# All query and key heads made as tile pairs in the projection stage of a gated linear attention encoder layer

## The chip, the cores and the metric

The kernel runs on one core of a Trainium2 chip. The time is the device time of one execution in microseconds (us), as the median of three runs. A profiled execution of the same program has a span (first to last instruction) and a time of its own.

## The reference, cut to what matters

One encoder layer runs over two sequences of 1024 tokens with 1024 features, in float32. For each sequence, with one weight matrix for all twelve projections:

```
h = rmsnorm(x, norm_g) * (1 + scale) + shift          # shift, scale, gate from silu(c) @ w_ada
a_b, a_c, a_x, a_z, q, k, v, b_z, lr_f, lr_b, m_a, m_b = split(h @ w_in)
y_a = (a_b * conv3(a_c * a_x) * silu(a_z)) @ w_a_out
g_f, g_b = log_sigmoid(lr @ w_gate + b_gate) / 16      # one decay per token and key feature
o   = gla(q, k, v, g_f) + reversed gla(q, k, v, g_b)   # 4 heads, 128 key and 256 value features
y_b = (rmsnorm(o) * gla_norm_g * silu(b_z)) @ w_b_out
y   = rmsnorm(x + gate * ((sigmoid(m_a) * y_a + sigmoid(m_b) * y_b) @ w_out))
```

Here gla is linear attention with a decay: token t sees an earlier token s through q_t, the product of the decays between the two, and k_s.

## The kernel before

**Precision.** Each factor of a large product is split into a high and a low part (`split`, L122 a copy on ScalarE, L123 a subtraction on VectorE), and three matmuls hi·hi, hi·lo and lo·hi make one product.

**Two kinds of dense product.** A weight tile gives 128 output features for all 1024 tokens. The plain way, `halves` and `group`, takes 48 matmuls of 512 columns for a tile (2 token halves, 8 blocks of the inner dimension, 3 parts), 96 for two tiles. `halves` hands them out in 4 steps of 12 matmuls; `group` takes two tiles at once and hands out one step for each of the 8 inner blocks. The pair way, `fast`, takes two tiles together by a Strassen-like scheme with 7 products of 12 matmuls, 84 for two tiles; `stationary` makes the 7 combined weight operands (VectorE and ScalarE) and, in the first sequence, also stores them in `kept_d`, from which `loaded` fetches them for the second sequence. Results are put together by VectorE and ScalarE behind each product.

**Stages.** For each sequence, `projections` runs a list of pair jobs: convolution tiles first, then one pair of Q tiles (heads 0 and 1), one pair of K tiles, four pairs each of V and of the gate b_z, four pairs of m_a. Beside the jobs behind the convolutions it hands out a side chain, `decays`, and in the second sequence `gate_rows`: `owed` grows with each product of a job, and a step of the chain is issued whenever it passes one. `decays` has a yield between its steps; for each head it loads `wg` and `lrs` from DRAM, then one step later multiplies them (L851), and works out the decays T over six more steps. The small product that `lrs` comes from is `low_ranks` (L818, 32 matmuls). `mixers` then runs the four heads of `attention`; between its parts it issues steps of dense products on the plain path, in proportion to a written length of each part (`LENGTHS`): first `gates` (Q and K tiles of heads 2 and 3, 16 steps; six m_b tiles, 24 steps; the last two as a `group`, 8 steps), then `first_out` (32 steps), which reads back the eight convolution results `ta_d` through `reload` (each in two halves, through the six `raw` buffers, split into eight of the 18 `big` buffers). That is 80 steps, 20 for a head. `merge` and, at the end, `final` follow.

**Inside a head.** `attention` loads T, q and k, forms own-token products, then goes through 7 levels: a ScalarE copy (L920), matmuls (L892), and VectorE work on the products and on Q, K and T (L925, L933, L936, L938). Behind the levels come transposes, states and outputs with short VectorE work.

**What sets the order.** A list scheduler places instructions on each engine's queue, by the order in which the program issues them and by its own estimate of when their inputs are ready; an engine then works through its queue in that order. Loads of weights get a higher priority (`load_w`). In the opening, `queue` fixes the order of loads by hand.

Of the kernel before, what the change touches and what calls it, by code (L numbers as in the profile page):

```python
# [11 lines left out]
F32 = mybir.dt.float32  # L12
# [5 lines left out]
P = 128  # L18
D = 1024
KT = D // P  # L20
# [37 lines left out]
def encoder_kernel(ctx, tc, x_p, x_s, x_t, weights, w_lr, w_gate, w_out, vectors, b_gate, final_norm_g, masks, y_p, y_s):  # L58
# [44 lines left out]
    kept_d = dram.tile([36, 7, P, 2 * HALF], F32, name="kept_d")  # L103
# [250 lines left out]
    def run(steps):  # L354
        for _ in steps:
            pass
# [59 lines left out]
    def start(mv):  # L416
# [12 lines left out]
        nc.scalar.activation(out=consts[:, 5:6], in_=sc[:, 0, :1], func=AF.Abs_reciprocal_sqrt, bias=eps)  # L429
# [4 lines left out]
        def tokens(i):  # L434

            sq = big("sq")
            for b in range(2):
                queue(nc.sync.dma_start(out=xT[i][:, b, :], in_=x_t[0, i + 4 * b]))
                nc.scalar.activation(out=sq[:, b, :], in_=xT[i][:, b, :], func=AF.Square)
            last = i == KT // 2 - 1  # L440
            if not last:
                nc.vector.tensor_add(out=sq[:, 0, :], in0=sq[:, 0, :], in1=sq[:, 1, :])
            over_features([sq[:, b, :] for b in range(1 + last)], lambda t: sums[t], i == 0, last)
# [150 lines left out]
    def projections(s, mv, started):  # L594
# [100 lines left out]

        for w, d in ((W_Q, q_d), (W_K, k_d)):
            jobs.append(out_job(w, [d[s][r, :, 0, :] for r in range(2)]))
# [7 lines left out]
        if not started:  # L705
            run(low_ranks(s, mv))
            more = last_conv_jobs(0)
            jobs = more + jobs
            n_conv += len(more)
        steps = 7 * (len(jobs) - n_conv)  # L710
        side = chain(decays(s), gate_rows() if s else ())
        n_side = (1 + 8 * NH) + (KT + 1 + 2 if s else 0)
        owed = 0.0
        for n, _ in enumerate(fast(jobs, mv)):
            if n + 1 >= 7 * n_conv:
# [34 lines left out]
    def mixers(s, mv):  # L750
        def gates():
            for w, d in ((W_Q, q_d), (W_K, k_d)):
                for h in range(2, NH):
                    sg = small("sg")
                    yield from halves(w + h, lambda ps, sl: nc.scalar.copy(out=sg[:, sl], in_=ps), mv.act)
                    nc.scalar.dma_start(out=d[s][h, :, 0, :], in_=sg)
# [13 lines left out]
            yield from group([(W_MA + i, gate(i)) for i in range(n, n + 2)], mv.act)  # L770

        def first_out():
            act = reload(ta_d[s])
# [21 lines left out]
        dense, each = chain(gates(), first_out()), (2 * KT + 4) * 4.0 / NH  # L795
        owed = 0.0
# [30 lines left out]
    def decays(s):  # L827
# [12 lines left out]
        for h in range(NH):  # L840
            wg, lrs = small("wg", F32R, (96, 2, P)), small("lrs", F32R, (96, L))
            nc.sync.dma_start(out=wg.bitcast(F32), in_=wg_d[:, :, h * P:(h + 1) * P])
            nc.sync.dma_start(out=lrs.bitcast(F32), in_=lr_d[s])
            yield
# [362 lines left out]
```

## Time and profile before

| | us |
|---|---|
| median of 3 runs | 2380.84 (2375.48 to 2383.9) |
| the profiled execution, its own time | 2388.54 |
| its span | 2386.7 |
| PE busy in the span | 2300.6 |
| DVE (VectorE) busy | 1422.5 |
| ACT (ScalarE) busy | 1002.8 |

PE is TensorE, PEld its weight loads, DVE VectorE, ACT ScalarE, POOL GpSimd and SP the queue that issues most loads. Matmuls overlap in the pipeline, so the duration of one is longer than the distance to the next, and a busy PE can still be slower than its best. PEclk is the clock granted to TensorE, 1.00 for 2.4 GHz and 0.50 for 1.2 GHz. L123 is line 123 of the kernel.

By the first instruction of each head on VectorE (L885), the heads of the first sequence begin at 673.6, 762.5, 851.7 and 957.7 us, those of the second at 1746.9, 1833.2, 1922.3 and 2029.3 us. L955, the first VectorE instruction behind the levels, falls at 804.2 us in the second head of the first sequence, and at 907.6 us in the third.

### The profile page before, as it was taken

How to read it: one execution, taken by the hardware profiler on the slowest of the kernel's cores; microseconds unless marked ns; L12 is line 12 of the kernel's file. 1: busy time of each engine (PE TensorE's matmuls, PEld its weight loads, DVE VectorE, ACT ScalarE, POOL GpSimd, SP SyncE). 2: the span in 40 equal slices, each digit the busy share in tenths (PEclk: the TensorE clock that was granted, in tenths of full speed). 3: DMA queues.
4: the chain of work that ended last, by engine and by line, in shares of the span. 5: the costliest groups of instructions: out<-in, count | busy, mean ns of one | idle time of the engine just before them, and what ended most of it. 6: DMA issues, size and time to landing. Idle time of an engine off the chain costs nothing.

```text
span 2386.7 us, 29259 instructions
## 1 busy us (share of the span) xinstructions
PE 2300.6 (96%) x10897; PEld 1882.3 (79%) x10897; DVE 1422.5 (60%) x2021; ACT 1002.8 (42%) x1652; POOL 35.7 (1%) x72
## 2 busy tenths in 40 slices
PE   7999999999989989999899999999999989999998
PEld 3688887887878877888688888878788868888887
DVE  4666776666676787967632332333576776955443
ACT  4543333566745545543421113544245444442221
POOL 0000000000000000000000000000000000000000
PEclk9999999999999999999999999999999999999999
DMA  6167767888853245565356666778854144468431
GB/s 236 67 250 278 269 256 279 308 302 304 315 203 137 76 144 202 210 236 198 113 203 212 210 207 225 258 255 278 293 192 154 58 157 167 153 232 308 157 124 62
DMA packets 189902, 494.63 MB, mean 207 GB/s; under 512 B 18912, under 2 KB 45632, under 8 KB 185664
## 3 DMA queue, kind: packets, MB, share of 16 engines
q1 hardware_dynamic: 166960, 405.98, 49.2%
q10 hardware_dynamic: 22800, 86.78, 9.5%
q8 instruction: 86, 1.41, 0.2%
q14 instruction: 56, 0.46, 0.1%
HBM read 294.90 MB, written 197.79 MB: 206 GB/s over the span
## 4 chain that ended last, share of the span: by engine, by line
PE 81%; DVE 7%; DMA 6%; ACT 3%; issue 1%; SPq 1%; POOL 0%; DVEq 0%; POOLq 0%; ACTq 0%
PE ps L141 9%; PE ps L143 9%; PE ps L142 9%; PE pl L277 8%; PE pl L278 8%; PE pl L279 8%; PE ps L277 6%; PE ps L278 6%; PE ps L279 6%; PE pl L892 2%; DMA raw<-in_weights_dram 2%; PE pm L141 1%; PE pm L142 1%; PE pm L143 1%; PE pm L413 1%
## 5 line engine op out<-in xcount | busy, mean ns | idle before, releaser
L123 DVE TENSOR_TENSOR w<-raw,w 128x512 fp32r<-128x512 f32 x298 | 201.9, 686 | 124.7 <-ACT w L122 123.6
L122 ACT CAST w<-raw 128x512 fp32r<-128x512 f32 x298 | 183.8, 621 | 143.6 <-PE ps L143 44.3
L277 PE MATMUL pl<-th,w 128*128 128x512 f32 x584 | 227.8, 390 | 0.0
L278 PE MATMUL pl<-tl,w 128*128 128x512 f32 x584 | 227.5, 390 | 0.0
L279 PE MATMUL pl<-th,w 128*128 128x512 f32 x584 | 227.4, 389 | 0.0
L141 PE MATMUL ps<-b,w 128*128 128x512 f32 x512 | 203.8, 398 | 16.0 <-ACT w L122 16.0
L142 PE MATMUL ps<-b,w 128*128 128x512 f32 x512 | 201.9, 394 | 0.0
L143 PE MATMUL ps<-b,w 128*128 128x512 f32 x512 | 201.9, 394 | 0.0
L141 PE MATMUL ps<-hi,w 128*128 128x512 f32 x432 | 173.2, 401 | 1.7 <-ACT hi L390 1.7
L282 ACT COPY keep<-pl 128x512 f32<-128x512 f32 x116 | 67.6, 583 | 254.8 <-PE pl L279 254.7
L143 PE MATMUL ps<-hi,w 128*128 128x512 f32 x432 | 172.1, 398 | 0.0
L142 PE MATMUL ps<-lo,w 128*128 128x512 f32 x432 | 171.2, 396 | 0.7 <-DVE lo L391 0.7
L277 PE MATMUL ps<-hi,w 128*128 128x512 f32 x352 | 137.6, 391 | 0.8 <-ACT w L122 0.8
L278 PE MATMUL ps<-lo,w 128*128 128x512 f32 x352 | 137.7, 391 | 0.0
L279 PE MATMUL ps<-hi,w 128*128 128x512 f32 x352 | 137.6, 391 | 0.0
L277 PEld LDWEIGHTS pl<-th,w 128*128 128x128 f32 x584 | 109.7, 188 | 23.9 <-ACT keep L282 0.7
L278 PEld LDWEIGHTS pl<-tl,w 128*128 128x128 f32 x584 | 109.8, 188 | 22.9
L279 PEld LDWEIGHTS pl<-th,w 128*128 128x128 f32 x584 | 109.8, 188 | 22.9
L141 PEld LDWEIGHTS ps<-b,w 128*128 128x128 f32 x512 | 97.3, 190 | 34.8 <-ACT w L122 16.6
L143 PEld LDWEIGHTS ps<-b,w 128*128 128x128 f32 x512 | 97.0, 189 | 19.9 <-DVE w L123 0.5
L892 PEld LDWEIGHTS pl<-Q,km 128*128 128x128 f32 x768 | 94.3, 196 | 22.0 <-ACT km L920 11.1
L142 PEld LDWEIGHTS ps<-b,w 128*128 128x128 f32 x512 | 97.2, 190 | 18.1
(288 smaller groups left out, 5041.6 us busy)
## 6 DMA issues: line engine op xcount, KB each, us to landing
kept_d<-w SPq DMA_DIRECT2D x196, 512.0 KB, 4.0
raw<-in_weights_dram SPq DMA_DIRECT2D x256, 256.0 KB, 4.3
w<-kept_d SPq DMA_DIRECT2D x112, 512.0 KB, 3.7
wk<-kept_d SPq DMA_DIRECT2D x168, 256.0 KB, 3.1
g<-g_d SPq DMA_DIRECT2D x32, 512.0 KB, 4.8
araw<-in_weights_dram SPq DMA_DIRECT2D x16, 512.0 KB, 3.8
ta_d<-u ACTq DMA_DIRECT2D x16, 512.0 KB, 3.6
v_d<-single ACTq DMA_DIRECT2D x16, 512.0 KB, 4.9
```

Of the source, the lines that this page charges most:

```text
L122: high = nc.scalar.copy(out=hi, in_=raw)
L123: engine.tensor_sub(out=lo, in0=raw, in1=hi.bitcast(F32))
L141: nc.tensor.matmul(out, ahi, bhi, start=(first and i == 0), stop=False)
L142: nc.tensor.matmul(out, ahi, blo, start=False, stop=False)
L143: nc.tensor.matmul(out, alo, bhi, start=False, stop=(last and i == n - 1))
L277: nc.tensor.matmul(ps, whi[:, cs], mhi, start=(first and k == 0), stop=False, skip_group_check=True)
L278: nc.tensor.matmul(ps, whi[:, cs], mlo, start=False, stop=False, skip_group_check=True)
L279: nc.tensor.matmul(ps, wlo[:, cs], mhi, start=False, stop=(k == 3), skip_group_check=True)
L282: nc.scalar.copy(out=job[i, "keep"], in_=ps)
L413: nc.tensor.matmul(ps[:2, :2 * P], sc[:, :, 4 * kg + k], raw[:, k, :], start=(kg + k == 0), stop=(kg * k == 3))
L892: nc.tensor.matmul(pl[:, j * P:(j + 1) * P], km[:, c * P:(c + 1) * P], qm(c), start=True, stop=True)
```

## The change

- The Q and K tiles of heads 2 and 3 leave `gates` (16 steps of the plain path for each sequence) and become two more pair jobs in `projections`: 16 pair jobs behind the convolutions in place of 14, and four more entries in `kept_d`.
- `mixers` has 64 dense steps in place of 80, 16 for a head, and begins with `owed = 2.0`.
- The reload of the convolution results moves from the start of `first_out` into the last `group` of `gates`: two tiles behind each of its last four steps.
- `decays` gets one more yield between the loads of `wg` and `lrs` and their first use; the side chain's count goes from 8 to 9 steps a head.
- In the second sequence, `low_ranks` is issued behind the ninth product of the pair jobs, not ahead of the first.
- In the opening, the first Square (L439) must follow the one-element Abs_reciprocal_sqrt (L429), and so the Sigmoid ahead of that one.

```diff
-    kept_d = dram.tile([36, 7, P, 2 * HALF], F32, name="kept_d")
+    kept_d = dram.tile([40, 7, P, 2 * HALF], F32, name="kept_d")
...
-        nc.scalar.activation(out=consts[:, 5:6], in_=sc[:, 0, :1], func=AF.Abs_reciprocal_sqrt, bias=eps)
+        table = nc.scalar.activation(out=consts[:, 5:6], in_=sc[:, 0, :1], func=AF.Abs_reciprocal_sqrt, bias=eps)
...
-                nc.scalar.activation(out=sq[:, b, :], in_=xT[i][:, b, :], func=AF.Square)
+                square = nc.scalar.activation(out=sq[:, b, :], in_=xT[i][:, b, :], func=AF.Square)
+                if i + b == 0:
+                    after(square, table)
...
         for w, d in ((W_Q, q_d), (W_K, k_d)):
-            jobs.append(out_job(w, [d[s][r, :, 0, :] for r in range(2)]))
+            for h in range(0, NH, 2):
+                jobs.append(out_job(w + h, [d[s][h + r, :, 0, :] for r in range(2)]))
...
         if not started:
-            run(low_ranks(s, mv))
             more = last_conv_jobs(0)
...
-        n_side = (1 + 8 * NH) + (KT + 1 + 2 if s else 0)
+        n_side = (1 + 9 * NH) + (KT + 1 + 2 if s else 0)
         owed = 0.0
         for n, _ in enumerate(fast(jobs, mv)):
+            if s and n == 8:
+                run(low_ranks(s, mv))
...
         def gates():
-            for w, d in ((W_Q, q_d), (W_K, k_d)):
-                for h in range(2, NH):
-                    sg = small("sg")
-                    yield from halves(w + h, lambda ps, sl: nc.scalar.copy(out=sg[:, sl], in_=ps), mv.act)
-                    nc.scalar.dma_start(out=d[s][h, :, 0, :], in_=sg)
...
-            yield from group([(W_MA + i, gate(i)) for i in range(n, n + 2)], mv.act)
+
+            for k, _ in enumerate(group([(W_MA + i, gate(i)) for i in range(n, n + 2)], mv.act)):
+                if k >= 4:
+                    reload(ta_d[s], conv, (2 * k - 8, 2 * k - 7))
+                yield
+
+        conv = [None] * KT
 
         def first_out():
-            act = reload(ta_d[s])
+            def act(k, sl):
+                return conv[k][:, 0, sl], conv[k][:, 1, sl]
...
-        dense, each = chain(gates(), first_out()), (2 * KT + 4) * 4.0 / NH
-        owed = 0.0
+        dense, each = chain(gates(), first_out()), 2 * KT * 4.0 / NH
+        owed = 2.0
...
             nc.sync.dma_start(out=lrs.bitcast(F32), in_=lr_d[s])
+            yield
             yield
             t1, t2 = big("t1"), big("t2")
```

## Rows read from the trace of the kernel before

**Rows 1.** Windows (start:end, length, busy us and count by engine), undisturbed projections of both sequences.

```profile
440.00:540.00 100.00, 100.00 (x443) 82.70 (x442) 67.72 (x95) 59.08 (x80) 0.00 (x0) 1.00 0.86 321
...
1180.00:1460.00 280.00, 280.00 (x1237) 231.86 (x1236) 86.96 (x93) 52.88 (x76) 0.00 (x0) 1.00 0.60 205
```

**Rows 2.** Windows: PE, PEld, DVE, ACT, POOL, then PEclk, DMA share; heads in two stretches.

```profile
762.50:804.20 41.70, 41.41 (x232) 35.08 (x230) 38.78 (x51) 19.03 (x32) 0.00 (x0) 1.00 0.39 147
804.20:851.70 47.50, 46.99 (x276) 39.94 (x275) 27.07 (x48) 25.52 (x60) 2.40 (x4) 1.00 0.28 94
851.70:907.60 55.90, 43.05 (x221) 35.47 (x220) 48.35 (x67) 27.90 (x48) 0.00 (x0) 0.88 0.56 198
907.60:957.70 50.10, 48.97 (x285) 41.32 (x284) 38.55 (x69) 29.64 (x68) 3.02 (x4) 1.00 0.49 165
...
1922.30:1979.30 57.00, 44.62 (x220) 37.02 (x219) 48.45 (x68) 27.61 (x48) 0.00 (x0) 0.85 0.55 194
```

**Rows 3.** Windows of the dense products' tile ps alone (PE, PEld, DVE, ACT), second head.

```profile
762.50:804.20 41.70, 29.61 (x120) 22.02 (x120) 0.00 (x0) 2.83 (x5) 1.00 0.39 147
804.20:851.70 47.50, 30.99 (x122) 21.78 (x122) 0.00 (x0) 3.10 (x6) 1.00 0.28 94
```

**Rows 4.** Groups by line of VectorE, 762.5 to 804.2 us: weight splits.

```profile
L123 DVE TENSOR_TENSOR w<-raw,w 128x512 fp32r<-128x512 f32 x5 | 3.4, 686 | 0.0
```

**Rows 5.** The chain of waits: PE, the whole span; us in total, times, longest.

```profile
PE ps L141 <- ACT w L122: 16.0, 2, 8.3
PE pm L851 <- DMA lrs<-lr_d: 11.1, 4, 3.8
PE pm L413 <- POOL sc L426: 7.4, 1, 7.4
PE pl L370 <- ACT Xh L122: 6.9, 2, 6.7
...
PE pm L1035 <- DVE ot L1027: 5.7, 11, 0.6
...
PE ps L818 <- ACT hi L122: 4.1, 1, 4.1
```

**Rows 6.** Groups by line of VectorE, 851.7 to 907.6 us: splits of the reload.

```profile
L123 DVE TENSOR_TENSOR b<-raw,b 128x512 fp32r<-128x512 f32 x16 | 10.6, 683 | 0.0
```

**Rows 7.** Waits of the SP queue, 851 to 907 us.

```profile
SPq L117 <- DVE b L123: 28.4, 12, 8.1
```

**Rows 8.** Windows (columns as in Rows 2) around the four waits for lrs.

```profile
400.00:420.00 20.00, 16.40 (x66) 13.09 (x65) 10.31 (x15) 6.98 (x12) 0.00 (x0) 0.91 0.91 314
540.00:560.00 20.00, 17.58 (x71) 14.01 (x70) 9.32 (x15) 12.39 (x20) 0.00 (x0) 0.91 0.80 294
1560.00:1580.00 20.00, 16.22 (x65) 12.90 (x64) 2.07 (x3) 3.59 (x6) 0.00 (x0) 0.91 0.81 263
1620.00:1640.00 20.00, 18.74 (x83) 15.20 (x82) 4.43 (x5) 12.49 (x16) 0.00 (x0) 1.00 0.79 255
```

**Rows 9.** Timeline of ScalarE in the opening: start, us, instruction.

```profile
7.55 1.06 ACT L439 ACTIVATE sq<-xT 128x1024 f32<-128x1024 f32 x1 [5.55 <-DMA xT<-in_x_t_dram]
8.63 1.28 ACT L425 ACT_TABLE_LOAD   x1
...
11.06 1.28 ACT L429 ACT_TABLE_LOAD   x1
...
12.56 5.77 ACT L439 ACTIVATE sq<-xT 128x1024 f32<-128x1024 f32 x6
```

**Rows 10.** Timeline of PE in the opening.

```profile
10.46 6.28 PE L413 MATMUL pm<-araw,sc 128*2 128x256 f32 x16 [7.44 <-POOL sc L426]
...
22.54 7.11 PE L370 MATMUL pl<-sq,ones 128*128 128x512 f32 x12 [1.64 <-DVE sq L442]
```

**Rows 11.** Page, DMA issues: count, KB each, median us to landing.

```profile
v_d<-single ACTq DMA_DIRECT2D x16, 512.0 KB, 4.9
```

**Rows 12.** Windows (columns as in Rows 2), two us inside the third head's wait.

```profile
896.00:898.00 2.00, 0.00 (x0) 0.00 (x0) 0.22 (x1) 0.00 (x0) 0.00 (x0) 0.50 1.02 349
```

## The prediction

> **What bounds the kernel now.** I read the share of each engine first, then windows stage by stage, then the waits of TensorE, then single stretches. TensorE is the bound nearly everywhere: in undisturbed stretches of the projections it never pauses, with 443 matmuls in 100 us or 1237 in 280 us [rows 1]. That is 0.226 us from one to the next, and it is the price of a 512-column matmul in all that follows (a single one is shown as 0.39 us, because neighbours overlap). VectorE and ScalarE have room there: 67.7 and 59.1 us of 100 in the first sequence, far less in the second.
>
> The heads of the attention are different, and the reader should see two stretches in each [rows 2]. From the head's first VectorE instruction to the end of the levels, 41.7 us in the second head, VectorE is busy for 38.8 us (93%) and TensorE for 41.4: both are full. From there to the next head, 47.5 us, VectorE is busy for 27.1 us only and TensorE for 47.0. The dense steps are spread evenly: 120 matmuls in the first stretch and 122 in the second [rows 3], about what the program's written lengths ask for (43 of 83 parts of 240). So the scheduler does not run dense work ahead to any extent that shows.
>
> **What leaves and what comes, on TensorE.** Four more pair jobs (two for each sequence) are 4 x 84 = 336 matmuls, at 0.226 us +76.0 us, all in stages where TensorE has no gap to hide them. VectorE and ScalarE keep up with such jobs today [rows 1], so I add nothing for the operands and the stores. Eight tiles leave the attention, 8 x 48 = 384 matmuls, 86.9 us if TensorE stays the bound there. On TensorE alone the change is worth 10.9 us.
>
> **What the attention gives back.** Each of eight heads loses 48 matmuls, about 24 in each stretch. In the second stretch VectorE leaves 20 us free, so 24 x 0.226 = 5.4 us come back, 43 us over eight heads. In the first VectorE is as full as TensorE; all that comes back is what the missing tile asked of VectorE: two splits of 0.686 us a head, half of them in this stretch [rows 4], 0.7 us, 5.5 us in all. TensorE will then idle for some 4.7 us in each first stretch. Lower bound 49 us, upper bound 87 us if the scheduler lets later dense steps run ahead into the gaps and the second stretch shrinks in turn. I take the lower one, because the even counts of [rows 3] show no run-ahead. From it I take 6 us: in the second stretch TensorE already waits for the scaled output, 5.7 us in 11 waits [rows 5], each behind a few dense matmuls, and with a fifth fewer of them I let these waits double. Net -43 us.
>
> **The reload.** The third heads last 106.0 and 107.0 us against 88.9 to 89.2 for undisturbed neighbours (from the heads' first instructions), 17 us too long each. In their first stretches, 55.9 and 57.0 us, VectorE works for 48 us and TensorE is at a mean clock of 0.88 and 0.85 [rows 2]. The cause: 16 reload splits, 10.6 us of VectorE [rows 6], fall into the stretch where it has nothing to spare, and the first weights of `first_out` wait in SP's queue behind raw buffers that these splits hold (28.4 us in 12 waits [rows 7]). TensorE then stands for 8.3 us and again in the second sequence, 16.0 us together [rows 5]. After the change the four reload steps are dense steps 29 to 32; with 16 a head and a start of 2 they fall at (29-2)/16 = 1.69 to 1.88 heads, in the second stretch of the second head. There VectorE has 20 us free for 11 us, and the buffers of the projections' operands come free one pair with each step. What may still be late is the weights of `first_out`, four raws behind sixteen in the same six buffers, issued in the last step; and the loads of T, q and k for the third head queue on SP behind them. I let 5 us of the 17 stay in each sequence: -25 us. Bounds: -10 (the weights are still as late as a whole wait of 8 us) and -34.
>
> **The decays.** At four places TensorE waits for `lrs`, 11.1 us in all, 3.8 the longest [rows 5]. The matmuls missing around them, against 89 in 20 us, are 23, 18, 24 and 6 [rows 8], 71 x 0.226 = 16 us, because the granted clock is lower behind each wait (0.91 on average in three of the windows). The added yield gives the loads one more side step. There are 48 or 37 steps for 112 products, so one in 2.3 to 3.0 products of 2.7 us: 6.3 to 8 us more, above the longest wait. I take -15. Bounds: -8 (half of the waits move on with the load, which can itself be late on SP) and -16. The same chain has `gate_rows`; its spacing hardly changes and I leave its waits alone.
>
> **The opening.** The Sigmoid stands behind the first Square, which waits until 7.55 us for its data, and behind a table load of 1.28 us; a second one comes at 11.06 [rows 9]. So `sc` is late and TensorE starts the conditioning product at 10.46 us, after 7.4 us of waiting [rows 5, 10]. With the small functions first, that product can start some 4 us earlier, and both table loads are gone from among the squares; the last square can end little earlier, as its data arrive late. The sums end at 29.7 us today [rows 10] and everything behind follows them. I take -5, between 0 and -7.
>
> **Low ranks and the start of the heads.** Moving `low_ranks` takes away 32 matmuls (7.2 us) with which TensorE partly fills the time until the last normalised tile is there; it waits for that tile inside them now (4.1 us [rows 5]). Other products of the first pairs can take part of the place: +2, between -3 and +5. Its weights take one of four operand buffers for some products; the pair jobs have six operands made ahead, so I add nothing. At the first head of the first sequence TensorE waits 6.7 us for the own-token operand [rows 5]; `owed = 2.0` puts two more dense steps (5.4 us) ahead of it, but the queue already holds three there. -2, between 0 and -5.
>
> **The sum.** 76 - 43 - 25 - 15 - 5 + 2 - 2 = -12 us. Against the profiled execution's own 2388.5 that is 2376.5; the median shown lies 7.7 us below that execution, so I forecast 2369 us. A change of 0.3%, 7 us, is about what a measurement of this kernel can tell from none.
>
> **The rivals.**
> *The dense work runs ahead.* The scheduler fills the gaps of the first stretches, and nearly all of the 87 us come back: 38 to 44 us more than I count, about 2328 us. For it: ahead of the first head's own products, TensorE did run dense steps while it waited. Against it: [rows 3].
> *The reload stays a stall.* The move doesn't do what it says, since the weights of `first_out` still come behind the reload's raws in SP's queue [rows 7], or T, q and k behind both; then the 25 us are not gained: 2394 us, slower. It decides from 12 us of 25 on.
> *Small buffers run short.* `wg` and `lrs` hold two of six `small` buffers for a side step longer, while two to four hold results on their way out and one the temporary of a silu. When none is free, the copy out of a product waits, and TensorE behind it. A store needs 4.9 us to land [rows 11]; one such wait for each of eight head loads is 39 us: 2408 us. It decides from 1.5 us a load on. Against it: the waits of TensorE list none on a store.
> *The clock.* Inside the long waits the granted clock fell to 0.50, that is 1.2 GHz [rows 12], while the many short waits in the second head went with 1.00 [rows 2]. If the gaps of 4.7 us a head, spread over seven levels, bring the lower level, one first stretch at 1.2 GHz doubles some 36 us of TensorE's work (41.4 less 24 matmuls), 31 us longer after its slack; one in eight is enough to be slower, 2400 us. The Trainium skill ("TensorE: Matmul & The Clock Gate", section "A second HAM failure mode: psum-queue depth-cycling") says that brief idling between groups of matmuls, if frequent, can make the clock swing between its levels; by that rule this rival would be the likeliest case. The trace doesn't bear it out so far: 11 waits of up to 0.6 us fell in stretches at 1.00.
>
> **How the numbers follow.** Forecast 0.46, within 2356 to 2382 by its own bounds; run-ahead 0.22; reload stays 0.12; small buffers 0.10; clock 0.04; 0.06 for what I don't see. Faster by over 0.3% (under 2373.7) are two thirds of the first, all of the second and a few others: 0.58. Same: the rest of the first, some of the third: 0.21. Slower 0.21. The range of 8 in 10 reaches from the run-ahead case to the reload that stays: 2328 to 2395.
>
> **What would show it.** Right: heads with 96 dense matmuls in each stretch, a first stretch still near 41 us with TensorE idle for 4 to 5, a second near 42; third heads below 92 us; no wait for `lrs`; the conditioning product starting before 7 us; two jobs more of 19 us in each projection stage. Wrong: first stretches with 110 or more dense matmuls and heads near 79 us (run-ahead); TensorE still waiting for the weights of `first_out`; new waits on stores in the projections; a clock below 1.00 in the levels.

## The result and the profile after

The changed kernel takes 2400.2 us (median of 4 runs, 2395.3 to 2401.2), against 2382.37 for the kernel before on the same chip. The medians are 17.8 us apart; the ratio over the runs is 1.0064, with a 95% interval of 1.0048 to 1.008, which is some 15 us. It is slower, where 12 us less was forecast, and it lies outside the range. Its profiled execution has a span of 2397.6 us, 10.9 more than the one before, which was itself 6 us above its median.

The page after, its head:

```profile
span 2397.6 us, 29218 instructions
...
PE 2304.7 (96%) x10849; PEld 1885.0 (79%) x10849; DVE 1435.3 (60%) x2043; ACT 995.6 (42%) x1645; POOL 36.0 (1%) x72
```

Cut at the same events in both traces (first pair product, first VectorE instruction of the first head, last VectorE output of the last head, first pair product of the next projections or first product of `final`), the spans divide as follows.

| stage | before, us | after, us | difference |
|---|---|---|---|
| opening, to the first pair product | 118.3 | 114.5 | -3.8 |
| projections, first sequence | 555.3 | 586.5 | +31.2 |
| attention, first sequence | 375.2 | 357.3 | -17.9 |
| merge, first sequence | 89.3 | 83.5 | -5.8 |
| projections, second sequence | 608.9 | 643.3 | +34.4 |
| attention, second sequence | 372.3 | 349.4 | -22.9 |
| merge, second sequence | 85.5 | 81.4 | -4.1 |
| final | 181.9 | 181.6 | -0.3 |

The projections grew by 65.6 us, and attention and merge gave back 50.7. One thing lies between the two: in the kernel before, the low-rank product of the second sequence begins 84.0 us into the 89.3 of the first merge row, so 5.3 us of that row's 5.8 are the moved product, which the kernel after has in its projections. Counted with that product in the projections both times, these grew by 60 us, where the sum had 63 (76 - 15 + 2), and attention and merge gave back 45, where it had 70 (43 + 25 + 2). Nearly the whole error stands in that one place. That the projections come so near is luck in part: the runs below show two of their terms off in opposite directions. The windows of the kernel after, with the columns of [rows 2], show what its attention stage is made of; the first two lines are the two attention stages, then come seven of its sixteen stretches:

```profile
701.10:1058.40 357.30, 322.62 (x1806) 273.33 (x1806) 294.72 (x452) 187.68 (x383) 10.48 (x16) 0.95 0.43 153
1785.10:2134.50 349.40, 321.35 (x1804) 272.49 (x1804) 283.33 (x433) 175.09 (x361) 10.50 (x16) 0.96 0.40 141
...
743.80:785.50 41.70, 40.94 (x246) 34.91 (x245) 27.41 (x49) 23.75 (x57) 2.44 (x4) 1.00 0.29 101
785.50:826.80 41.30, 40.56 (x233) 33.85 (x232) 39.32 (x54) 20.66 (x34) 0.00 (x0) 1.00 0.34 128
826.80:876.60 49.80, 42.42 (x239) 36.14 (x238) 34.32 (x62) 29.26 (x71) 2.52 (x4) 0.93 0.57 195
876.60:921.40 44.80, 40.85 (x230) 35.01 (x228) 42.90 (x60) 23.34 (x38) 0.00 (x0) 0.96 0.37 137
921.40:969.20 47.80, 42.73 (x238) 35.61 (x238) 37.92 (x68) 28.27 (x65) 2.40 (x4) 1.00 0.58 190
...
1013.10:1058.40 45.30, 32.44 (x166) 27.71 (x165) 34.67 (x61) 24.83 (x60) 3.12 (x4) 0.77 0.42 140
2089.10:2134.50 45.40, 33.33 (x166) 28.39 (x165) 34.58 (x61) 24.81 (x60) 3.12 (x4) 0.77 0.41 139
```

The reader should see three things. The third head's first stretch did fall, from 55.9 us [rows 2] to 44.8. The second head's second stretch did not: 47.5 us before [rows 2], 49.8 now, though it holds fewer dense matmuls. And the last heads' second stretches take 45 us with TensorE busy for 32 or 33 of them. The dense products alone (tile ps) in those two last stretches:

```profile
1013.10:1058.40 45.30, 8.75 (x35) 6.08 (x34) 2.61 (x4) 0.00 (x0) 0.77 0.42 140
2089.10:2134.50 45.40, 8.69 (x35) 6.21 (x34) 2.75 (x4) 0.00 (x0) 0.77 0.41 139
```

33 of these 35 begin inside the stretch, where an even spread has 96, and only 7 and 8 of them are dense steps of the attention stage, all in its first 2 us. The other 26 and 25 are products of merge, behind a pause of some 30 us. The dense work has run ahead and is used up; what lasts is the chain of short steps of the last head alone. TensorE's clock falls there (columns as above):

```profile
1015.00:1020.00 5.00, 0.87 (x7) 0.78 (x7) 5.00 (x6) 2.02 (x4) 0.00 (x0) 0.98 0.26 105
1020.00:1033.00 13.00, 10.17 (x42) 8.66 (x41) 9.03 (x22) 5.79 (x15) 0.00 (x0) 0.50 0.11 42
```

TensorE was busy for 0.87 us of 5 before the clock fell to 1.2 GHz, and then worked for 10.17 of 13 us at that level.

The head of the list of TensorE's waits, after, whole span:

```profile
PE pm L1041 <- DVE ot L1033: 23.5, 12, 4.7
PE pm L977 <- DVE kt L123: 8.3, 2, 4.1
PE pl L370 <- ACT Xh L122: 6.9, 2, 3.7
PE pl L370 <- DVE sq L444: 4.6, 2, 3.0
```

The waits for `lrs` (11.1 us) and for the first weights of `first_out` (16.0 us) of [rows 5] are gone. In their place TensorE waits 23.5 us for the scaled output `ot`, 5.7 before [rows 5]; the three longest waits are now for steps of the heads' own chain. The cause in the second head is seen in the groups of VectorE from 826.8 to 876.6 us (first its busy time, then the idle time before and what ended it) and in the issues of SP there:

```profile
L123 DVE TENSOR_TENSOR b<-raw,b 128x512 fp32r<-128x512 f32 x16 | 10.6, 685 | 0.8 <-ACT b L122 0.7
...
L1033 DVE TENSOR_TENSOR ot<-ot,ors 128x1024 f32<-128x1024 f32 x2 | 2.4, 1224 | 6.0 <-POOL ors L363 6.0
```

```profile
837.86 12.03 SPq L117 DMA_DIRECT2D raw<-ta_d  x10
851.36 6.20 SPq L117 DMA_DIRECT2D raw<-in_weights_dram  x6
859.43 2.94 SPq L117 DMA_DIRECT2D raw<-in_x_t_dram  x3
862.42 0.90 SPq L782 DMA_DIRECT2D g<-g_d  x2
863.72 0.32 SPq L883 DMA_DIRECT2D T<-t_d  x1
866.15 0.32 SPq L885 DMA_DIRECT2D qk<-q_d  x1
```

All 16 splits of the reload fall into this one stretch, where the prediction had put them, between the short VectorE steps on which the states and outputs wait. Behind the reload on SP come weights, the next normalisation's input, and only then T and q of the third head, whose first ScalarE step waits 6.4 us for q.

### The profile page after: what moved, and what is told of

Same layout as the page of the kernel before. It is cut to its first block, busy times and chain, and to the rows that moved or that the text cites. A ratio compares the mean times of both kernels' runs of the same rounds, so it can differ in the third digit from the quotient of the medians.

```text
span 2397.6 us, 29218 instructions
## 1 busy us (share of the span) xinstructions
PE 2304.7 (96%) x10849; PEld 1885.0 (79%) x10849; DVE 1435.3 (60%) x2043; ACT 995.6 (42%) x1645; POOL 36.0 (1%) x72
## 4 chain that ended last, share of the span: by engine, by line
PE 79%; DVE 7%; DMA 6%; ACT 4%; issue 2%; POOL 1%; SPq 0%; DVEq 0%; ACTq 0%; POOLq 0%
PE ps L141 9%; PE ps L143 9%; PE ps L142 9%; PE pl L279 8%; PE pl L277 8%; PE pl L278 8%; PE ps L279 6%; PE ps L278 6%; PE ps L277 6%; PE pl L898 3%; DMA raw<-in_weights_dram 3%; PE pm L141 1%; PE pm L142 1%; PE pm L143 1%; PE pl L370 1%
## 5 line engine op out<-in xcount | busy, mean ns | idle before, releaser
L277 PE MATMUL pl<-th,w 128*128 128x512 f32 x624 | 244.6, 392 | 0.3 <-ACT keep L282 0.3
L279 PE MATMUL pl<-th,w 128*128 128x512 f32 x624 | 244.2, 391 | 0.0
L278 PE MATMUL pl<-tl,w 128*128 128x512 f32 x624 | 244.0, 391 | 0.0
L279 PE MATMUL ps<-hi,w 128*128 128x512 f32 x376 | 146.5, 390 | 0.4 <-DVE w L123 0.4
L278 PE MATMUL ps<-lo,w 128*128 128x512 f32 x376 | 146.5, 390 | 0.4 <-DVE lo L123 0.4
L277 PE MATMUL ps<-hi,w 128*128 128x512 f32 x376 | 146.5, 390 | 0.4 <-ACT hi L122 0.4
L277 PEld LDWEIGHTS pl<-th,w 128*128 128x128 f32 x624 | 117.8, 189 | 26.3 <-ACT keep L282 0.9
L278 PEld LDWEIGHTS pl<-tl,w 128*128 128x128 f32 x624 | 117.9, 189 | 24.7
L279 PEld LDWEIGHTS pl<-th,w 128*128 128x128 f32 x624 | 117.8, 189 | 24.7
L141 PE MATMUL ps<-hi,w 128*128 128x512 f32 x304 | 123.4, 406 | 1.7 <-ACT hi L390 1.7
L142 PE MATMUL ps<-lo,w 128*128 128x512 f32 x304 | 121.3, 399 | 0.7 <-DVE lo L391 0.7
L143 PE MATMUL ps<-hi,w 128*128 128x512 f32 x304 | 121.1, 398 | 0.0
```

The source lines that it names most:

```text
L141: nc.tensor.matmul(out, ahi, bhi, start=(first and i == 0), stop=False)
L142: nc.tensor.matmul(out, ahi, blo, start=False, stop=False)
L143: nc.tensor.matmul(out, alo, bhi, start=False, stop=(last and i == n - 1))
L277: nc.tensor.matmul(ps, whi[:, cs], mhi, start=(first and k == 0), stop=False, skip_group_check=True)
L278: nc.tensor.matmul(ps, whi[:, cs], mlo, start=False, stop=False, skip_group_check=True)
L279: nc.tensor.matmul(ps, wlo[:, cs], mhi, start=False, stop=(k == 3), skip_group_check=True)
```

## The experiments

Two theories stood after the comparison. The first: the heads are bound by their own chain once 16 dense steps a head are left, so that what is taken off TensorE or VectorE there comes back only in part. The second: the heads could be shorter, but something of the change is badly placed (the reload, the raw buffers, dense work that runs ahead). Ratios are to the kernel before, on the same chip, with 95% intervals.

### Which part costs what

**The pairs alone** on the kernel before (the jobs, the steps taken out of `gates`, `each`):

```diff
-            jobs.append(out_job(w, [d[s][r, :, 0, :] for r in range(2)]))
+            for h in range(0, NH, 2):
+                jobs.append(out_job(w + h, [d[s][h + r, :, 0, :] for r in range(2)]))
...
-        dense, each = chain(gates(), first_out()), (2 * KT + 4) * 4.0 / NH
+        dense, each = chain(gates(), first_out()), 2 * KT * 4.0 / NH
```

> The kernel before with only the Q and K tiles moved into pair jobs (64 dense steps, start of 0; reload, decays, opening and low ranks as before). Theory A, the attention gives back about half of the 87 us that leave it while the four jobs cost 76: 2405 to 2420 us, with the third heads' stall still there. Rival B, the pairs pay and one of the moved parts costs: 2360 to 2378 us.

Measured: 2408.1 us, 1.0102 [1.0081, 1.0122]. The projections grow by 34.1 and 34.7 us (68.8, against 76 by count), attention and merge fall by 43.8 together. So the pairs lose some 25 us by themselves, and the rest of the change gives only 9 of them back. The two attention stages, with the columns of [rows 2], and the wait for `lrs` that is left:

```profile
708.70:1072.50 363.80, 325.84 (x1803) 274.20 (x1802) 295.90 (x452) 188.53 (x383) 10.35 (x16) 0.94 0.43 151
1801.00:2149.40 348.40, 320.62 (x1815) 271.09 (x1814) 284.10 (x433) 175.91 (x362) 10.89 (x16) 0.96 0.40 141
```

```profile
PE pm L847 <- DMA lrs<-lr_d: 3.9, 2, 3.6
```

The last line tells why the jobs cost 69 us and not 76. In the projections, TensorE's busy time grows by 74 us (1142 to 1216), near the count; its pauses shrink by 5.5, as the side chain's steps are spread over 112 products of jobs in place of 98, and the waits for `lrs` fall from 11.1 us [rows 5] to 3.9.

Two things more stand in this trace. The reload's splits fall between 876 and 895 us, behind the start of the third head, and the wait for the first weights of `first_out` stays (14.3 us). And neighbouring heads overlap: the third head's first VectorE instruction comes at 860.3 us, 23.9 behind the end of the second head's levels, while the second head's last output follows at 883.6. So the length of a head from start to start (68.7 us here, then 122.9) belongs to the order that the scheduler chose; the stages are no shorter for it.

**The small parts alone** (opening, extra yield, moved low-rank product):

> The kernel before with the opening's order, the added yield of the decays and the moved low ranks, and nothing else. Theory A: the waits for lrs (16 us with the slow clock) and some 5 us of the opening go: 2355 to 2365 us. Rival B, these parts cost as much as they bring: 2376 to 2390 us.

Measured: 2374.8 us, 0.9957 [0.9943, 0.9971], 10 us less, where the prediction's terms make 18. By these ratios the pairs and the small parts make 1.0059 together, and the whole change 1.0064: the moved reload and the owed start, which were to bring 27 us, brought nothing that can be measured.

**The yield alone:**

```diff
-        n_side = (1 + 8 * NH) + (KT + 1 + 2 if s else 0)
+        n_side = (1 + 9 * NH) + (KT + 1 + 2 if s else 0)
...
             nc.sync.dma_start(out=lrs.bitcast(F32), in_=lr_d[s])
             yield
+            yield
```

> The kernel before with only the added yield of the decays and its count. The prediction's term: 15 us less, ratio 0.9937, the waits for lrs gone. Rival: the three small parts together gave 10 us, of which the opening is 4 by its stage, and one wait for lrs was still there (2.4 us); so 6 to 8 us, ratio 0.997, and the waits are shorter rather than gone, for lrs is late on SP by more than one side step.

Measured: 0.9978 [0.9969, 0.9988], 5 us less. Its waits of TensorE:

```profile
PE ps L141 <- ACT w L122: 15.2, 2, 8.7
...
PE pm L370 <- ACT gp L122: 5.4, 1, 5.4
...
PE ps L277 <- ACT w L205: 3.2, 1, 3.2
PE pm L852 <- DMA lrs<-lr_d: 3.1, 1, 3.1
```

Three of the four waits for `lrs` are gone (11.1 us before [rows 5], 3.1 now), but two others have come, which the kernel before does not list among its longest: 5.4 us for the operand of `gate_rows`, issued from the same side chain, and 3.2 us for a pair job's operand. Both fall in the projections. The prediction had left `gate_rows` alone.

**The changed kernel without the four added jobs** (queries and keys of heads 2 and 3 are not made; those of heads 0 and 1 are read):

> The changed kernel without the four added pair jobs: Q and K of heads 2 and 3 are not made, and those of heads 0 and 1 are read in their place. By the sum, 4 x 84 matmuls of 0.226 us: 76 us less than the changed kernel, 2324 us. If jobs cost more than their matmuls (operands, stores, the side chain): 2315 us or less. If part of them filled waits: 2332 us or more.

Measured: 2335.6 us, 0.981 [0.9781, 0.984]: 61 us below the kernel after by the ratios, 64 by its projections (559.0 and 606.9 us). The jobs cost 61 to 69 us in these runs, not 76. Without them, waits like those of the yield alone stand in the projections (5.4 us for `gate_rows`, 3.5 for a pair job's operand, 2.5 for `lrs`), which are 1.1 us or less in the kernel after.

### Whether dense work that runs ahead starves the last head

**Dense steps held back:** the first matmul of a dense step must follow the last matmul that attention issued before it.

```diff
+        if not pe["dense"]:
+            pe["mine"] = made
+        elif pe["due"]:
+            after(made, pe["mine"])
+            pe["due"] = False
```

> The changed kernel with an order on TensorE's queue: no dense step of the attention stage stands ahead of the attention matmuls issued before it. Theory A, dense work run ahead starves the last head (31 dense matmuls in its second stretch, TensorE idle for 22 us): the last heads get some 100 dense matmuls back and end 4 to 8 us sooner each, while TensorE idles more in first stretches: 2385 to 2395 us. Rival C, the second stretches are bound by their own chain whatever the filling: 2398 to 2410 us.

Measured: 2456.6 us, 1.0305 [1.0276, 1.0333]. The last heads do get about 200 dense matmuls each, but the heads last 89.7 to 101.6 us, where they had 83.9 to 92.6. TensorE's waits, first two lines:

```profile
PE pl L140 <- ACT Xh L122: 31.8, 8, 5.0
PE pl L140 <- ACT km L940: 21.8, 16, 3.5
```

Held back in this way, dense matmuls no longer cover the latencies of the chain. Running ahead is not the fault.

**More work for the last head:** the first 72 matmuls of merge, with the reload of six tiles that they need, become six more dense steps, 17.5 for a head in place of 16; they are the last ones, at the end of the last head.

```diff
-        dense, each = chain(gates(), first_out()), 2 * KT * 4.0 / NH
+        dense, each = chain(gates(), first_out(), first_merge()), (2 * KT * 4.0 + 6) / NH
```

> The changed kernel, with the first 72 matmuls of merge (two output tiles over the first six inner blocks, and the reload of those blocks) issued as 6 more dense steps in the last head. Theory A: they fill idle time of the last head's second stretch, 16 us for each sequence less what the reload adds: 2370 to 2382 us. Rival C, TensorE's idle time there is not to be had because ScalarE, VectorE or the buffers hold the reload back: 2395 us or more.

Measured: 2441.1 us, 1.0235 [1.0215, 1.0255]. The last heads grow from 89.1 and 89.6 us to 99.3 and 94.9, and the two attention stages by 40 us together. TensorE also waits 18.2 us for copies of a reload, right behind the last heads, where merge has lost the products that it began with. TensorE's idle time in the last head was not to be had in this way, for work that needs VectorE and ScalarE as well.

### Whether the reload stands in the wrong place

**The reload back at the start of `first_out`**, the rest as after:

> The changed kernel with the reload of the convolution results back at the start of first_out, all else as changed. Theory D, the moved reload brings nothing because its loads, copies and splits hold up the second head's states and the third head's loads instead of first_out's weights: 2395 to 2408 us, within 6 us of the changed kernel. Rival, the move is worth the 25 us that the sum gave it and something else is lost: 2420 us or more.

Measured: 2394.5 us, 1.0049 [1.003, 1.0068], against 1.0064 for the kernel after: the move gains nothing that can be measured. The scheduler puts the reload into the second head's second stretch anyway (47.0 us; its splits fall between 849 and 867).

**Without raw buffers:** each tile is loaded whole into the low half of its big buffer and split in place, so that SP never waits for a raw buffer there.

```diff
-            for t in range(2):
-                sl = slice(t * HALF, (t + 1) * HALF)
-                split(b[:, 0, sl], b[:, 1, sl], staged(src[k][:, sl]), nc.vector)
+            whole = b.bitcast(F32)[:, 1, :]
+            nc.sync.dma_start(out=whole, in_=src[k])
+            split(b[:, 0, :], b[:, 1, :], whole, nc.vector)
```

On the kernel after:

> The changed kernel, but reload (that of merge too) loads each tile whole into the low half of its own big buffer and splits it there: no raw buffers and half the loads on SP, and one copy and one subtraction of 1024 columns in place of two of 512. Theory D1, the queue of SP and the six raw buffers are what holds up the neighbours: 2375 to 2390 us. Theory D2, the work on ScalarE and VectorE in between the states is: 2393 to 2402 us.

Measured: 2395.9 us, 1.0059 [1.0043, 1.0076]; the second stretch is 50.4 us. The same edit on the kernel before:

> The kernel before with the same reload without raw buffers, at its old place. If the wait of the third heads comes from first_out's weights behind the raw buffers of the reload, some 8 us for each sequence go: 2362 to 2374 us. If it comes from VectorE being full in that stretch, as much of the stall stays: 2376 to 2386 us.

Measured: 2370.6 us, 0.9958 [0.9943, 0.9973]. The third heads fall from 106.0 and 107.0 us to 99.9 and 99.8, and the wait for the first weights of `first_out` is gone from the list. So the queue of raw buffers cost something before, and nothing after.

**Without the split at all,** in the reload of the convolution results alone:

```diff
+            if any(src is d for d in ta_d):
+                for part in range(2):
+                    nc.sync.dma_start(out=b.bitcast(F32)[:, part, :], in_=src[k])
+                tiles[k] = b
+                continue
```

On the kernel after, before, and on the pairs alone:

> The kernel after, but the reload of the convolution results copies each tile by DMA into both halves of its big buffer; the split into high and low parts (16 copies on ScalarE and 16 subtractions on VectorE for each sequence) and the raw buffers are left out, so the low part is wrong data. The reload of merge keeps its split. Theory E (the engine work lengthens the chain at whatever place it stands): the second heads' second stretch falls from 49.8 and 49.7 us to some 42, the third heads' first from 44.8 to some 42, and the third heads lose the wait for q: 8 + 4 us for each sequence, about 2376 us, ratio 0.997 to before. Rival T (what is late is the transfers and SP's queue, the engines' work is hidden): 2394 to 2402 us, ratio 1.005 to 1.008, with second stretches still near 50 us.

> The kernel before with the same edit (no split in the reload of the convolution results). If the reload's work was the cause of the long third heads, as the prediction had it, they fall from 106 and 107 us to some 90, 34 us in all: 2350 us, ratio 0.986. If the transfers are the cause, they fall little: 2370 to 2382 us. The difference between this run and the kernel before is the reload's price there; the same difference for the kernel after, by theory E some 24 us, is what is left of it behind the move. The prediction had 34 and 9.

> The pairs alone, with the reload of the convolution results copied by DMA into both halves of its buffers; the split of it is left out, so the low part is wrong data. Theory F (the two gains are not additive): the reload's price is some 8 us here, as in the kernel after, so 2400 us, ratio 1.007. Rival (another part of the change makes the price small, and the terms add): 26 us, as in the kernel before, 2382 us, ratio 0.999.

Measured: after 1.0045 [1.0032, 1.0057], before 0.989 [0.9874, 0.9906], pairs alone 1.0119 [1.0095, 1.0143]. The windows of both attention stages, in this order: the kernel before, then it without the split; after, without the split (with it, above); the pairs alone, without the split.

```profile
673.60:1048.80 375.20, 352.23 (x1976) 297.50 (x1977) 300.68 (x460) 197.54 (x399) 11.13 (x16) 0.97 0.44 152
1746.90:2119.20 372.30, 355.35 (x1987) 299.88 (x1986) 288.06 (x439) 183.80 (x376) 9.60 (x16) 0.98 0.40 141
```

```profile
669.30:1030.90 361.60, 350.15 (x1982) 295.42 (x1981) 291.67 (x444) 188.43 (x383) 10.73 (x16) 1.00 0.48 170
1724.20:2083.60 359.40, 351.94 (x1986) 297.17 (x1985) 278.81 (x423) 175.22 (x360) 9.60 (x16) 1.00 0.44 157
```

```profile
708.90:1064.20 355.30, 324.03 (x1806) 273.34 (x1805) 285.67 (x436) 179.97 (x367) 10.36 (x16) 0.96 0.46 166
1786.10:2131.20 345.10, 318.25 (x1802) 269.50 (x1801) 273.99 (x417) 166.82 (x345) 10.44 (x16) 0.97 0.43 155
```

```profile
710.80:1075.10 364.30, 325.88 (x1807) 275.55 (x1806) 284.83 (x436) 178.55 (x367) 11.87 (x16) 0.95 0.45 162
1802.70:2153.80 351.10, 321.37 (x1805) 271.90 (x1804) 273.60 (x417) 166.85 (x345) 11.80 (x16) 0.97 0.42 151
```

Summed over both sequences:

| attention, us | with the split | without | the split's price |
|---|---|---|---|
| 20 dense steps a head (before) | 747.5 | 721.0 | 26.5 |
| 16 dense steps, pairs alone | 712.2 | 715.4 | -3.2 |
| 16 dense steps, the kernel after | 706.7 | 700.4 | 6.3 |

With 20 steps a head the reload costs what the prediction took off for it. (The price is that of the splits and of the raw buffers that go with them; the in-place reload, which keeps the splits, had 736.2 us.) With 16 it costs next to nothing, in the third head's first stretch (pairs alone) as in the second head's second, and the stages together stay between 700 and 715 us. Read down, the table says the same of the steps: without the split, four steps fewer a head bring 5.6 or 20.6 us, not 43. I had expected more (second stretches near 42 us in the kernel after): they fell to 44.8 and 46.0, but in the first sequence the third head's first stretch grew from 44.8 to 49.0, so the gain was lost again one stretch on.

### How long the heads are by themselves

**All dense steps behind the last head,** the first of their matmuls ordered behind its last one, nothing left out:

```diff
-                owed += each * length / LENGTH
+                continue
...
+        pe["dense"], pe["due"] = True, True
         run(dense)
```

> The kernel after with nothing left out, but all dense steps of the attention stage issued behind the last head, the first of them ordered behind the last head's last matmul. It shows how long the heads are by themselves. Theory F (with 48 matmuls fewer the heads of the kernel after are at the length of their own chain): bare heads of 78 to 84 us against 84 to 93 with 16 dense steps; four of them and 64 steps of 2.7 us behind give some 330 + 174 us for the stage, about 2700 us in all, ratio 1.13. Rival Q (the heads are long because dense steps stand in their queues): bare heads of 55 to 70 us, stage 430, 2550 us, ratio 1.07.

Measured: 2762.6 us, 1.1584 [1.1564, 1.1603]. Two heads of it in two stretches each, and its longest waits of TensorE:

```profile
798.90:844.10 45.20, 23.63 (x127) 20.45 (x127) 37.24 (x49) 16.22 (x27) 0.00 (x0) 0.75 0.13 52
844.10:885.60 41.50, 23.50 (x131) 20.66 (x131) 22.95 (x41) 17.63 (x45) 2.40 (x4) 0.77 0.20 63
885.60:932.80 47.20, 25.85 (x127) 22.45 (x127) 37.25 (x49) 16.32 (x27) 0.00 (x0) 0.66 0.14 57
932.80:974.30 41.50, 23.54 (x131) 20.73 (x131) 22.95 (x41) 17.63 (x45) 2.40 (x4) 0.77 0.19 65
```

```profile
PE pl L140 <- ACT Xh L122: 79.0, 8, 12.8
PE pm L992 <- DVE kt L123: 52.4, 8, 6.5
PE pm L1056 <- DVE ot L1048: 47.1, 16, 3.3
```

Without dense matmuls the eight heads take 86.7 to 90.2 us, longer than either forecast and about the same as the 83.9 to 92.6 us with 16 dense steps each. The second stretch is 40 to 43 us, though VectorE is busy for 23 us of it and TensorE for 24: neither engine fills it, it is a chain. There is a catch: the granted clock is 0.66 to 0.77 in these heads. TensorE has about 40% of the chain of waits from 885 to 975 us, some 36 us; if all of that ran at 2.4 GHz in place of a mean of 0.71, 10 us would go. So 78 us is an estimate of the least length of a head in this order, and 88 what it takes with the clock of this run.

### GpSimd for the subtractions

The reload's subtractions on GpSimd (`nc.vector` becomes `nc.gpsimd` in its `split`), on the kernel after; the same on the kernel before with the in-place reload; and, on the kernel after, those of `load_w`:

> The changed kernel, with the subtraction of reload's splits (32 for each sequence) on GpSimd in place of VectorE. Theory E, the heads of the changed kernel are as long as VectorE's work (90% busy in the attention stages) and the reloads lie in between: 22 us less work on VectorE for each sequence, 2365 to 2390 us. Rival F, the second stretches are as long as their chain of small steps whatever VectorE has beside it, or GpSimd's subtraction is late itself: 2396 us or more.

> The kernel before with the reload without raw buffers and its subtractions on GpSimd. Theory E says that what is left of the third heads' stall (99.9 against 89 us) is VectorE's full first stretch: another 8 to 10 us for each sequence, 2350 to 2362 us. If GpSimd's subtraction is slower than the group that needs it: 2372 us or more.

> The changed kernel, with the subtraction of load_w's splits (the weights of all dense steps and of merge) on GpSimd. Theory E: 16 tiles x 2 x 0.686 us leave VectorE in each attention stage, 22 us each, and weights are a few steps ahead of their use: 2365 to 2390 us. Rival F: 2396 us or more, with TensorE waiting for weights if GpSimd's subtraction is slow.

Measured: 2413.5 us, 1.0117 [1.0096, 1.0138]; 2413.0 us, 1.0117 [1.0094, 1.0141]; 2428.4 us, 1.0181 [1.0161, 1.02]. All three are slower than the kernels that they start from. The operations take twice as long there, and TensorE's waits for the scaled output, whose scale GpSimd makes too, grow: from 23.5 us to 34.3 in the first of the three. Theory E had VectorE at 90% in the attention stages; the windows above have 82 and 81%. The figures are in the last section.

### What to keep

The kernel before with the opening, the yield, the moved low-rank product and the in-place reload, without the pairs:

> The kernel before with the opening's order, the added yield, the moved low ranks and the reload without raw buffers, without the pairs. If the gains of the two runs (10 and 11 us) add up: 2358 to 2364 us. If they share the same wait: 2366 to 2374 us.

Measured: 2368.6 us, 0.9925 [0.9901, 0.9948]. It beats both kernels; the gains of its parts (0.9957 and 0.9958) add up. Of TensorE's waits it lists 3.1 us for `lrs` and 3.4 us for `gate_rows` still.

## Why the prediction was wrong

**What bounds the stages.** Right for the projections. For the heads it was half right: "both are full" holds for the first stretch of a head with 20 steps. The second stretch was read as bound by TensorE with 20 us of VectorE to spare. It is nearly as long as its chain: 47.5 us with dense work before [rows 2], 40 to 43 bare. The 42 us that the prediction expected there are already this length, and leave nothing for a reload.

**The jobs, +76.** Measured 69 by the projections of the pairs alone. The direction is right, the price a tenth high, and the difference was paid by the waits for `lrs`, which the prediction counted under the decays. Net of what attention gives back, +33 was predicted for the pairs and +25 measured.

**The attention gives back 43, and the reload 25.** This is the step that failed. Each term alone is near the truth: the pairs alone gave 43.8 with the merges, and the reload was worth 26.5 us before. But the sum adds them, to 68, and the attention stages gave back 40.8. Both were paid out of the same thing: the prediction let 24 matmuls leave the second stretch because VectorE "leaves 20 us free" there, and then put the reload's 11 us of splits into the same stretch because VectorE "has 20 us free for 11 us". The table of the split shows that they overlap: with the steps gone, the reload is worth 6 us or less. The allowance of 6 us for the scaled output, with waits that double, was too small as well: they went from 5.7 us to 23.5, and to 22.2 with the pairs alone. In the traces, the third heads became 13.4 and 21.9 us shorter (106.0 to 92.6, 107.0 to 85.1), where the prediction had 12 each from the reload and 5 from the steps; the first heads 4.5 and 2.4; but the second heads 1.9 and 1.7 longer, since the reload fell there, and the last heads 2.0 and 0.3 shorter.

By TensorE's books it comes out the same way. The windows of the two attention stages hold 353 matmuls fewer (3963 and 3610; the rest of the 384 is made up by products of merge that now run in the last heads), 80 us at 0.226. TensorE's busy time fell by 64 us only (707.6 to 644.0), and the time in which it is not busy grew by 23 (39.9 to 62.7), which leaves the 41. The 16 us between 80 and 64 fit the clock: TensorE is busy at 1.2 GHz for 51 us of these stages after the change and for 19 before, and half of the difference is 16. The bound of 49 us that the prediction called the lower one was none, alone or joined with the reload.

**The reload's place.** The four steps fell where they were worked out to fall, and the wait for the first weights of `first_out` went. But the move of the code did none of this by itself: with the reload back in `first_out` the time is the same within the intervals. The scheduler's own order had already made the choice.

**The decays, -15.** The waits for `lrs` are gone in the kernel after, as predicted, but the pairs alone take most of them (11.1 to 3.9 us), and the yield alone is worth 5 us (3 to 7): with it two other waits come up, one of them in the side chain. The term was mis-sized by 10 us and falls short of its own lower bound of 8.

**The opening, -5.** Right: -3.8. The conditioning product starts at 5.24 us, as these lines show, and the sums end at 25.2 us instead of 29.7 [rows 10]. But only the Sigmoid's table load has left the squares. One Square still runs ahead of the Abs_reciprocal_sqrt, whose table load follows it (the last line, of ScalarE).

```profile
5.24 5.66 PE L413 MATMUL pm<-araw,sc 128*2 128x256 f32 x16 [2.13 <-DMA araw<-in_weights_dram]
...
18.04 7.13 PE L370 MATMUL pl<-sq,ones 128*128 128x512 f32 x16 [1.64 <-DVE sq L444]
...
10.03 1.28 ACT L429 ACT_TABLE_LOAD   x1
```

**Low ranks and the owed start, +2 and -2.** Too small to be told apart. The small parts together less the yield and the opening leave -1 for the low ranks.

**The rivals.** "The dense work runs ahead" happened, without its price: the last heads' second stretches are left with 33 dense matmuls in 45 us, most of them merge's, because the chain is what lasts. "The reload stays a stall" comes nearest, 2394 us forecast, but its mechanism was another one: the weights are no longer late, and taking the reload's work away helps little. "Small buffers" did not happen: no wait on a store is among TensorE's longest. "The clock" did not come where it was feared: the first stretches are at 0.96 and 1.00. It came in second stretches (0.93 and 0.77), where TensorE has too little left to do, and it fits the 16 us of TensorE's time above. Of the work at 1.2 GHz, 43 us stand on the chain of waits in the attention stages, 19 before; half of the difference, 12 us, is an estimate of what the stages lost by it. No run tested it, and for second stretches the prediction had no price. The rule of the Trainium skill that was weighed there ("TensorE: Matmul & The Clock Gate", section "A second HAM failure mode: psum-queue depth-cycling") is borne out by the bare heads, where TensorE pauses at every level and has 0.66 to 0.77, and by the last heads' second stretches, where it goes from 0.98 to 0.50 in the rows above; in the other stretches, with 16 dense steps between the pauses, it has 0.93 to 1.00.

**What stays open.** How far below 88 us a head's chain would be with some dense work, but at the full clock; how much of what attention failed to give back is the clock, and how much the chain at any clock; and how much heads could overlap in another order. That the two stages can't go under 700 us together by freeing engines is shown for the reload's work alone.

## What to carry to other kernels

Before two gains in one stage are added, ask what bounds the stage after the first: the second may be paid out of the same idle time, and a run of each alone and of both tells it. A stretch with two engines at half load is not free room if its steps wait for each other in turn; its length without the filler work, in the same order, tells about how far it can shrink, and dense work taken out of it returned little below that here. Work that fills such gaps cost half of its time where it was, here 44 of 87 us; moved to a stage where its engine never pauses, it cost 74, of which 5 came back from shorter waits.

## What the runs showed of the hardware

A subtraction of 128x512 elements from SBUF takes 1420 ns on GpSimd where VectorE takes 683 [rows 6], and VectorE's own steps with both inputs in SBUF become slower beside it. The group of the kernel after with the reload on GpSimd, and then VectorE's groups of the kernel before with its in-place reload there (the last line is the kernel before itself):

```profile
L123 POOL TENSOR_TENSOR b<-raw,b 128x512 fp32r<-128x512 f32 x64 | 88.9, 1420 | 271.1 <-ACT b L122 270.7 <-DMA raw<-ob_d 0.3
```

```profile
L936 DVE TENSOR_TENSOR K<-K,T 128x512 f32<-128x512 f32 x112 | 90.7, 837 | 7.4 <-ACT km L920 5.3
...
L925 DVE COPY_PREDICATED AT<-mk,pl 128x512 f32<-128x512 uint8 x80 | 56.2, 732 | 6.6 <-PE pl L370 2.9 <-PE pl L892 2.8 <-ACT sg L761 0.4
...
L936 DVE TENSOR_TENSOR K<-K,T 128x512 f32<-128x512 f32 x112 | 73.7, 684 | 5.2 <-ACT km L920 3.5
```

The product K with T, both in SBUF, takes 837 ns on average there, 684 in the kernel before; the copy of products from the accumulators (AT) stays at 732, against 733. The Trainium skill says that the two engines share a pair of SBUF ports that one operation holds alone ("SBUF — State Buffer", section "Who interferes with whom"), and that an elementwise operation with two inputs is about twice as slow on GpSimd ("GPSIMD Engine Reference", section "4.1 Engine selection"). Both agree with these rows.
